# Attention scores: the keys' low-part product on all 128 rows, against tiles whose other half is zeros

## The chip, the cores and the metric

The kernel runs on one core of one Trainium2 chip. The core has a matrix engine (TensorE, PE in the profile, its weight loads listed as PEld), a vector engine (VectorE, DVE), a scalar engine (ScalarE, ACT), GpSimd (POOL) and a queue that issues transfers (SyncE, SP). The metric is the device time of one launch in microseconds (us), less is better. Before the change it is 1499.1 us, the median of three runs (1493.78 to 1500.56).

## The reference

A two-layer decoder trunk for 512 tokens of width 1024 with 16 learned meta tokens in front, so 528 positions. Layer 0 mixes an mLSTM head group and an RG-LRU branch; layer 1 is differential attention with 8 heads; a squared-ReLU MLP follows each layer. The change lies in the scores of layer 1:

```python
C_HEADS = D_MODEL // 128           # 8
C_QK_DIM = D_MODEL // (2 * C_HEADS)  # 64
Q_BLOCK = 128

def _diff_attend(qb, q_pos, kh, vh, k_pos, lam):
    """qb: (B,H,2,Lq,d), kh: (B,H,2,Lk,d), vh: (B,H,Lk,dv)."""
    s = jnp.einsum('bhcqd,bhckd->bhcqk', qb, kh)
    mask = k_pos[None, :] <= q_pos[:, None]
    p = jax.nn.softmax(jnp.where(mask, s, -jnp.inf), axis=-1)
    pd = p[:, :, 0] - lam * p[:, :, 1]
    return jnp.einsum('bhqk,bhkv->bhqv', pd, vh)
```

Every head has two components `c`, each with its own 64 query and key features, and the score is the plain dot product over these 64 features.

## The kernel before

All products are done on values split in two: a high part that TensorE's fast float format holds exactly, and the low part that is left. A product of two float32 values is then the sum of high x high, low x high and high x low. Weights come in 225 units of 128 x 1024 (`get_w`): a transfer, a cast to the high part on ScalarE (L157) and a subtraction for the low part on VectorE or, for a few units, GpSimd (L113). `unit_mm` (L188) multiplies a unit by the activations, three products for each of 8 blocks of rows.

Layer 1 goes head by head. `attend(hd)` runs three units for each head: queries, keys, values. Queries and keys get the rotary step (`raw`, `sh`, L740 to L743) and are split into `rh` and `rl` by `split` (L116 for the cast, and the subtraction by the helper at L113). Both components of a head lie on the 128 partitions, 64 each. Transfers then build for each component `c` a tile `st2[c]` of 128 rows: for queries the high part in the component's own half and the low part in the other half; for keys the high part in both halves. So one 128-row product of `qS[c]` and `kS[c]` (L792) gives high x high plus low x high. What is missing is the query's high part times the key's low part: a second product of 64 rows (L793), of the 64 rows of `qS[c]` that hold the query's high part and the 64 rows of `rl` of the keys that hold the component's low part. On the diagonal block a third product adds the causal mask (L796, `idr` times `mkr`, 128 columns). All three add up in one PSUM tile `psc`. VectorE takes the row maximum from it (`mx`, L798), turns it into the bias `nb` (L803), and ScalarE makes the exponentials (`e`, L806) which ends the use of `psc`.

A query block `I` of 128 queries sees 16 + 128 (I + 1) keys, so the score products have 144, 272, 400 or, in two parts, 2 x 264 columns. With two components that is 10 groups of products in each head, 2 of 144, 2 of 272, 2 of 400 and 4 of 264 columns, and 8 of them have the mask product.

The steps of a head (`s0` to `s3` scores, `t0` to `t3` transposes of the probabilities, `v` transposes of the values, `o` output, `f` its norm) are put between the units of the next two heads (`SLOTS`); the order within an engine is set by a scheduler that takes steps by priority groups. PSUM tiles of these steps come from a pool of four (`axp`); scratch rows come from a pool of 31 (`sc`).

Of the kernel before, what the change touches and what calls it, by code (L numbers as in the profile page):

```python
# [10 lines left out]
F32 = mybir.dt.float32  # L11
F32R = mybir.dt.float32r
# [4 lines left out]
P = 128  # L17
T = 528
# [24 lines left out]
# layer 0 before its output projection, in order: units of head h (q<h><i>: query, key and value blocks), the gate  # L43
# unit e, output-gate units o<c>, RG-LRU input and gate units c<b> and g<b>; steps without a unit: squares S and
# statistics N of the norm, gate rows A B C, RG-LRU gates G<b> and recurrences R<pair>; p<n>: n steps of the heads
# [7 lines left out]
# elementwise steps that GpSimd takes instead of VectorE  # L53
POOL_OPS = "Mm"
# weight units, by place in the order, whose low parts GpSimd computes
POOL_L = {5, 33, 43, 44, 52, 126, 140, 143, 149, 151, 155, 159, 161, 164}
N_S = 31
LOAD1 = 9
BOOST = 568
# groups of steps that come before what was emitted a little earlier  # L60
# [18 lines left out]
def trunk(tc, hT, wu, wri, pk, lv, rope, gf, out, probe=None):  # L79
    nc = tc.nc  # L80
# [6 lines left out]
    with ctx:  # L87
# [14 lines left out]
        def sc(name, dt=F32, w=T):  # L102
            """scratch row block"""
            return big.tile([P, T], dt, tag="s", name=name, bufs=N_S)

        def xt(name):
            """a pair of float32r tiles for an exact split"""
            hi = big.tile([P, T], F32R, tag="x", name=name + "h", bufs=32)
            lo = big.tile([P, T], F32R, tag="x", name=name + "l", bufs=32)
            return hi, lo  # L110
# [35 lines left out]
        def emit_load():  # L146
# [9 lines left out]
            with soon():  # L156
                nc.scalar.copy(wh, raw)  # L157
                eng = nc.gpsimd if i in POOL_L else nc.vector
                if u == U_GATE:
                    # few columns: their low parts lie beside them  # L160
                    hi, r = (a.rearrange("p (k c) -> p k c", k=KB) for a in (wh, raw))
                    sub(eng, hi[:, :, 64:100], r[:, :, 0:36], hi[:, :, 0:36].bitcast(F32))
                else:
                    sub(eng, wl, raw, wh.bitcast(F32))
# [10 lines left out]
        def unit_mm(u, x, lo=0, n=T, mid=None):  # L175
            """128 output features x n tokens, K = 1024."""
# [15 lines left out]
        # steps that follow a unit's own evacuation, emitted between later units  # L192
# [9 lines left out]
        def rsq_of(dst, v, fn, le=False, after=None, src=None):  # L202
            """dst = 1/sqrt(v): a table's value and one Newton step. src: where v comes from, as (sum, scale)."""
# [20 lines left out]
        def norm_x(h, gc, lo, tag, late=False):  # L224
            """x = h*g split exactly, and the squares of h summed over feature blocks."""
# [19 lines left out]
        def norm_r(terms, lo, tag, le=False):  # L245
            """rstd = 1/sqrt(mean(h^2)+eps) on all partitions."""
# [12 lines left out]
        # half of log1p(y) for y in [0, 1], as atanh(y/(2+y))  # L259
# [14 lines left out]
        # =================== layer 0: mLSTM heads ===================  # L274
# [16 lines left out]
        # rows on their way to another layout  # L291
# [6 lines left out]
        # column spans of the five decay blocks, packed in three rows  # L298
# [23 lines left out]
        def head_steps(hd, qk, vr):  # L322
            """the head's quadratic form, in steps"""
# [59 lines left out]
            # numerator and denominator; tokens in two spans  # L383
# [55 lines left out]
        def gate_rows():  # L439
            # gate pre-activations  # L440
# [10 lines left out]
            # columns of rstd by token block  # L451
# [11 lines left out]
        def gate_a():  # L463
            """log sigmoid of the forget gates, spread over the partitions"""
# [11 lines left out]
        def gate_b():  # L476
            """rows of the decay exponents"""
# [36 lines left out]
        # =================== layer 0: RG-LRU and output projection ===================  # L514
        # -8*softplus(-lambda) and its negative
# [106 lines left out]
        # output projection: the RG-LRU half while the last head finishes, then the mLSTM half  # L622
# [25 lines left out]
        # =================== squared-ReLU MLP ===================  # L648
# [27 lines left out]
        # =================== layer 1: differential attention ===================  # L676
# [4 lines left out]
        # lambda  # L681
# [15 lines left out]
        # causal mask of a diagonal block (query partition, key free)  # L697
# [15 lines left out]

        steps = []

        def slot(hd, i):
            """the steps that follow the unit: of head hd - 1 and, primed, of head hd - 2"""
# [5 lines left out]
        def attend(hd):  # L723
# [3 lines left out]
            for w in range(2):  # L727
# [16 lines left out]
                hl_ = (sc("rh", F32R), sc("rl", F32R))  # L744
                with pri("S"):
                    split(hl_, raw[:, lo:], slice(lo, T))
                # by component: the high part in its own half; the query's low part, or the key's high part again,
                # in the other half
# [5 lines left out]
                rot.append((st2, hl_[1]))  # L754
# [9 lines left out]
        def attn_steps(hd, rot, vr):  # L764
            (qS, _), (kS, kL) = rot
# [13 lines left out]
            def sstep(I):  # L779
# [4 lines left out]
                for c in range(2):  # L784
                    pr = slice(64 * c, 64 * c + 64)
# [5 lines left out]
                    for r, (d, s0, m) in enumerate(spans):  # L791
                        nc.tensor.matmul(d[:, :m], qS[c][:, qs], kS[c][:, s0:s0 + m], start=True, stop=False)  # L792
                        nc.tensor.matmul(d[:, :m], qS[c][pr, qs], kL[pr, s0:s0 + m], start=False,  # L793
# [83 lines left out]
        # output projection: heads 0-5 while the last heads finish, then heads 6-7  # L877
# [19 lines left out]
        # =================== last MLP and the final norm, tokens on partitions at the end ===================  # L897
# [4 lines left out]
        def turn_h(t):  # L902
            """the residual of 128 tokens, transposed"""
# [8 lines left out]
        def final_quarter(a):  # L912
            w = [get_w(N_UNIT - 8 + k) for k in range(KB)]
            for t in range(4):
                tk = slice(NM + t * P, NM + (t + 1) * P)
                turn_h(t)
                # spans of features; the first tokens go through the weights as they come
# [37 lines left out]
def lay_out(x, meta_tokens, norm_mix, norm_mlp, norm_final, ab_w_in, ab_if_bias, mlstm_norm, lru_conv_w, lru_conv_b,  # L955
# [63 lines left out]
    # rotary tables, from the shapes alone  # L1019
# [28 lines left out]
```

## Time and profile before

The profiled execution has a span of 1495.0 us from its first to its last instruction, 4.1 us under the median of the three runs.

| what | value |
|---|---|
| median of the runs | 1499.1 us |
| span of the profiled execution | 1495.0 us |
| TensorE busy | 1470.7 us, 98% |
| VectorE busy | 832.2 us, 56% |
| ScalarE busy | 634.8 us, 42% |
| GpSimd busy | 125.2 us, 8% |
| TensorE's mean granted clock | 0.993 |
| first and last score product (L792) | 856.6 us and 1083.9 us |

Shares over the whole span mix stages: VectorE, at 56% on average, is busy for eight tenths or more of most slices of the attention heads. In a timeline each row is an instruction or a run of equal ones, with its start and how long it is recorded; since matmuls overlap, what one costs is read from the start of one row to the start of the next.

### The profile page before, as it was taken

How to read it: one execution, taken by the hardware profiler on the slowest of the kernel's cores; microseconds unless marked ns; L12 is line 12 of the kernel's file. 1: busy time of each engine (PE TensorE's matmuls, PEld its weight loads, DVE VectorE, ACT ScalarE, POOL GpSimd, SP SyncE). 2: the span in 40 equal slices, each digit the busy share in tenths (PEclk: the TensorE clock that was granted, in tenths of full speed). 3: DMA queues.
4: the chain of work that ended last, by engine and by line, in shares of the span. 5: the costliest groups of instructions: out<-in, count | busy, mean ns of one | idle time of the engine just before them, and what ended most of it. 6: DMA issues, size and time to landing. Idle time of an engine off the chain costs nothing.

```text
span 1495.0 us, 24176 instructions
## 1 busy us (share of the span) xinstructions
PE 1470.7 (98%) x9970; PEld 1351.7 (90%) x9970; DVE 832.2 (56%) x1481; ACT 634.8 (42%) x1090; POOL 125.2 (8%) x94
## 2 busy tenths in 40 slices
PE   8999999999999999999999999999999999999998
PEld 8999999999999999999999888888777888888887
DVE  5867745667444434344344578888865434343452
ACT  6465734656334224132233445655645223132342
POOL 3000000100020000000003111111123000000001
PEclk9999999999999999999999989999999999999999
DMA  7332223232232232323223433222222323332331
GB/s 252 95 113 80 97 72 119 73 97 71 71 98 87 86 98 86 98 86 90 95 86 99 128 85 92 80 86 78 79 71 85 98 87 97 99 97 88 98 116 54
DMA packets 48794, 140.79 MB, mean 94 GB/s; under 512 B 9226, under 2 KB 10775, under 8 KB 48684
## 3 DMA queue, kind: packets, MB, share of 16 engines
q1 hardware_dynamic: 48108, 138.21, 30.3%
q8 instruction: 78, 1.28, 0.4%
q10 hardware_dynamic: 576, 1.05, 0.2%
q14 instruction: 32, 0.26, 0.1%
HBM read 128.55 MB, written 2.16 MB: 87 GB/s over the span
## 4 chain that ended last, share of the span: by engine, by line
PE 92%; DVE 3%; ACT 2%; issue 1%; DMA 1%; POOL 0%; SPq 0%; ACTq 0%; DVEq 0%; POOLq 0%
PE mm L188 76%; PE mf L927 3%; PE mo L890 3%; PE psc L793 2%; PE po L852 1%; PE pnum L391 1%; PE psc L796 1%; PE psc L792 1%; PE pg L584 1%; PE pss L373 1%; PE pt L828 1%; PE poq L862 0%; DVE wl L113 0%; PE pden L391 0%; ACT wh L157 0%
## 5 line engine op out<-in xcount | busy, mean ns | idle before, releaser
L157 ACT CAST wh<-raw 128x1024 fp32r<-128x1024 f32 x225 | 236.3, 1051 | 624.6 <-PE mm L188 516.0
L113 DVE TENSOR_TENSOR wl<-raw,wh 128x1024 fp32r<-128x1024 f32 x210 | 267.8, 1276 | 76.8 <-ACT wh L157 75.8
L671 DVE TENSOR_TENSOR h<-mm,h 128x264 f32<-128x264 f32 (+1 forms) x88 | 41.3, 499 | 188.3 <-PE mm L188 188.3
L241 POOL TENSOR_TENSOR nsq<-nsq 128x528 f32<-128x528 f32 (+1 forms) x28 | 48.5, 1731 | 451.0 <-DVE wl L113 336.3
L660 DVE SCALAR_TENSOR_TENSOR rt<-mm,mrstd 128x264 f32<-128x264 f32 x64 | 24.7, 427 | 88.8 <-PE mm L188 88.8
L660 DVE SCALAR_TENSOR_TENSOR rt<-mm,nrstd 128x512 f32<-128x512 f32 x32 | 22.1, 692 | 79.9 <-PE mm L188 79.8
L113 POOL TENSOR_TENSOR wl<-raw,wh 128x1024 fp32r<-128x1024 f32 x14 | 33.9, 2421 | 232.0 <-ACT wh L157 190.0
L798 DVE TENSOR_REDUCE mx<-psc 128x1 f32<-128x264 f32 (+3 forms) x80 | 34.4, 434 | 23.7 <-PE psc L796 18.1
L806 ACT ACTIVATE e<-psc,nb 128x264 f32<-128x264 f32 (+3 forms) x80 | 38.2, 482 | 18.8 <-DVE nb L803 17.7
L662 ACT ACTIVATE rt<-rt 128x528 f32<-128x528 f32 (+1 forms) x64 | 40.5, 635 | 3.1 <-DVE rt L660 2.8
L741 POOL TENSOR_TENSOR qr<-qr,tb 128x512 f32<-128x512 f32 (+1 forms) x16 | 26.4, 1648 | 156.5 <-DVE nb L803 90.7
L936 POOL TENSOR_TENSOR zg<-z,gfr 128x512 f32<-128x512 f32 x4 | 5.2, 1294 | 343.2 <-DVE z L934 332.5
L631 DVE TENSOR_TENSOR h<-mm,h 128x264 f32<-128x264 f32 x32 | 12.3, 427 | 38.5 <-PE mm L188 38.5
L840 ACT CAST pp<-pt 128x128 fp32r<-128x128 f32 (+2 forms) x64 | 21.0, 343 | 28.8 <-PE pt L828 16.7
L793 PE MATMUL psc<-rl,st 64*128 64x264 f32 (+3 forms) x80 | 31.7, 397 | 0.0
L116 ACT CAST rh<-qr 128x512 fp32r<-128x512 f32 (+1 forms) x16 | 10.0, 627 | 45.3 <-DVE qr L743 42.7
L793 PEld LDWEIGHTS psc<-rl,st 64*128 64x128 f32 x80 | 14.9, 187 | 15.0 <-issue 9.7
L188 PE MATMUL mm<-ax0h,wh 128*128 128x264 f32 x98 | 22.0, 297 | 6.1 <-ACT ax0h L230 6.1
L792 PE MATMUL psc<-st,st 128*128 128x264 f32 (+3 forms) x80 | 25.3, 317 | 2.6 <-DMA st<-rh 1.5
L113 DVE TENSOR_TENSOR pp<-pt,pp 128x256 fp32r<-128x256 f32 (+2 forms) x64 | 23.6, 378 | 1.4 <-ACT pp L840 1.3
L188 PE MATMUL mm<-a6h,wh 128*128 128x264 f32 (+1 forms) x88 | 22.6, 316 | 0.0
L188 PE MATMUL mm<-a4h,wl 128*128 128x264 f32 (+1 forms) x88 | 22.6, 316 | 0.0
(799 smaller groups left out, 4781.2 us busy)
## 6 DMA issues: line engine op xcount, KB each, us to landing
raw<-wu SPq DMA_DIRECT2D x225, 512.0 KB
h<-hT SPq DMA_DIRECT2D x16, 264.0 KB
st<-rh SPq DMA_DIRECT2D x32, 132.0 KB
st<-rh SPq DMA_DIRECT2D x16, 128.0 KB
st<-rl SPq DMA_DIRECT2D x16, 128.0 KB
cb<-crow SPq DMA_DIRECT2D x4, 264.0 KB
erb<-crow SPq DMA_DIRECT2D x4, 264.0 KB
rawg<-wri SPq DMA_DIRECT2D x4, 256.0 KB
```

The costliest lines, as they stand in the source:

```text
L113: eng.tensor_tensor(out=o, in0=a, in1=b, op=ALU.subtract)
L157: nc.scalar.copy(wh, raw)
L188: nc.tensor.matmul(p[:, :m], w[:, c], xx[:, s:s + m], start=(k == 0 and j == 0), stop=(k == KB - 1 and j == len(terms) - 1))
L241: nc.gpsimd.tensor_tensor(out=fin[0][:, lo:], in0=fin[0][:, lo:], in1=sq[:, lo:], op=ALU.add)
L660: nc.vector.scalar_tensor_tensor(out=t[:, tk], in0=p, scalar=0.0, in1=rs[:, tk], op0=ALU.max, op1=ALU.mult)
L662: nc.scalar.activation(out=t[:, lo:], in_=t[:, lo:], func=AF.Square)
L671: nc.vector.tensor_tensor(out=h[:, c, tk], in0=p, in1=h[:, c, tk], op=ALU.add)
L792: nc.tensor.matmul(d[:, :m], qS[c][:, qs], kS[c][:, s0:s0 + m], start=True, stop=False)
L793: nc.tensor.matmul(d[:, :m], qS[c][pr, qs], kL[pr, s0:s0 + m], start=False, stop=s0 + m != nk)
L806: nc.scalar.activation(out=e[:, s0:s0 + m], in_=d[:, :m], func=AF.Exp, bias=nb, scale=0.125, accum_out=ss[:, c + 2 * r:c + 2 * r + 1])
L890: nc.tensor.matmul(ps, w[ww][:, b], co[k][xx][:, NM:], start=(k == ks[0] and j == 0), stop=(k == ks[-1] and j == 2))
L927: nc.tensor.matmul(pss[n][:, :m], a[k][aa][:, tk], w[k][ww][:, f0:f0 + m], start=(k == 0 and i == 0), stop=(k == KB - 1 and i == 2))
```

## The change

The 64-row product becomes a 128-row one. Six tiles `kz` (three pairs, one of each pair for each component) are set up once; the half of a tile that belongs to the other component is filled with zeros by GpSimd. For the keys the subtraction that made the 128-row `rl` is replaced by two subtractions of 64 rows, each into the component's half of its `kz` tile; the pair is `hd % 3`. The second product then takes all 128 rows of `qS[c]` and of `kz[c]`: rows of the query's low part meet zeros. Nothing else of the computation changes; the keys no longer take an `rl` tile from the scratch pool. The rest of the diff removes comments.

```diff
+N_KZ = 3
...
+        kz = [[cp.tile([P, T], F32R, name=f"kz{i}{c}") for c in range(2)] for i in range(N_KZ)]
+        for pair in kz:
+            for c in range(2):
+                nc.gpsimd.memset(pair[c][64 - 64 * c:128 - 64 * c, :].bitcast(F32), 0.0)
...
-                hl_ = (sc("rh", F32R), sc("rl", F32R))
+                hl_ = (sc("rh", F32R), None if w else sc("rl", F32R))
                 with pri("S"):
-                    split(hl_, raw[:, lo:], slice(lo, T))
+                    if w:
+                        nc.scalar.copy(hl_[0], raw)
+                        for c in range(2):
+                            own = slice(64 * c, 64 * c + 64)
+                            sub(nc.vector, kz[hd % N_KZ][c][own, :], raw[own, :], hl_[0][own, :].bitcast(F32))
+                    else:
+                        split(hl_, raw[:, lo:], slice(lo, T))
...
-                rot.append((st2, hl_[1]))
+                rot.append(st2)
...
-            (qS, _), (kS, kL) = rot
+            qS, kS = rot
+            kL = kz[hd % N_KZ]
...
-                    pr = slice(64 * c, 64 * c + 64)
...
                         nc.tensor.matmul(d[:, :m], qS[c][:, qs], kS[c][:, s0:s0 + m], start=True, stop=False)
-                        nc.tensor.matmul(d[:, :m], qS[c][pr, qs], kL[pr, s0:s0 + m], start=False,
+                        nc.tensor.matmul(d[:, :m], qS[c][:, qs], kL[c][:, s0:s0 + m], start=False,
                                          stop=s0 + m != nk)
```

TensorE, the scores of one query block in a middle head (400 columns, both components); `mm` are a unit's products, `pt` the transposes behind. Before:

```order
L188 MATMUL mm_11290<-dx7h,wl_10995 128x512
L792 MATMUL psc<-st_11085,st_10948 128x400
L793 MATMUL psc<-rl,st_10948 128x400
L796 MATMUL psc<-mkr,idr 128x128
L792 MATMUL psc<-st_11086,st_10949 128x400
L793 MATMUL psc<-rl,st_10949 128x400
L796 MATMUL psc<-mkr,idr 128x128
L828 MATMUL pt<-ident,e_11183 72x128 x2
```

and now (the lines are 13 further down, or 2 for `unit_mm`):

```order
L190 MATMUL mm_11302<-dx7h,wl_11007 128x512
L805 MATMUL psc<-st_11097,st_10960 128x400
L806 MATMUL psc<-kz_9594,st_10960 128x400
L809 MATMUL psc<-mkr,idr 128x128
L805 MATMUL psc<-st_11098,st_10961 128x400
L806 MATMUL psc<-kz_9595,st_10961 128x400
L809 MATMUL psc<-mkr,idr 128x128
L841 MATMUL pt<-ident,e_11195 72x128 x2
```

The number and the order of TensorE's instructions stay; only the moving operand of the second product is another tile. (In the first three heads some groups of score products stand a few unit products earlier or later than before.)

VectorE in the same head, from the end of the keys' rotary step (`qr`) to the split of the values (`v1l`). Before:

```order
L743 TENSOR_TENSOR qr<-qr,qs 128x528
L815 TENSOR_SCALAR e_11037<-e_11037,rs_11044 128x272
L113 TENSOR_TENSOR pp<-pt,pp 72x2x128
L817 SCALAR_TENSOR_TENSOR e_11028<-e_11028,rs_11044,e_11037 128x272
L113 TENSOR_TENSOR rl<-qr,rh 128x528
L113 TENSOR_TENSOR v1l_11117<-pv_11119,v1h_11115 72x256
```

and now:

```order
L750 TENSOR_TENSOR qr<-qr,qs 128x528
L828 TENSOR_SCALAR e_11049<-e_11049,rs_11056 128x272
L115 TENSOR_TENSOR pp<-pt,pp 72x2x128
L830 SCALAR_TENSOR_TENSOR e_11040<-e_11040,rs_11056,e_11049 128x272
L115 TENSOR_TENSOR kz_9594<-qr,rh 64x528
L115 TENSOR_TENSOR kz_9595<-qr,rh 64x528
L115 TENSOR_TENSOR v1l_11129<-pv_11131,v1h_11127 72x256
```

One subtraction of 128 rows has become two of 64, and the split of the values stands one place later.

GpSimd at the start of the program (`nsq` are sums of squares for the first norm). Before:

```order
masks.py:197 MEMSET ident 128x128
masks.py:199 ISA
masks.py:199 AFFINE_SELECT ident<-ident 128x128
L241 TENSOR_TENSOR nsq<-nsq 128x528 x7
```

and now:

```order
masks.py:197 MEMSET ident 128x128
L719 MEMSET kz_9592 64x528
masks.py:199 ISA
masks.py:199 AFFINE_SELECT ident<-ident 128x128
L719 MEMSET kz_9593 64x528
L719 MEMSET kz_9594 64x528
L719 MEMSET kz_9595 64x528
L719 MEMSET kz_9596 64x528
L719 MEMSET kz_9597 64x528
L243 TENSOR_TENSOR nsq<-nsq 128x528 x7
```

The six fills stand ahead of the first sum of squares, one of them ahead of the last step of the identity matrix.

## Rows read from the trace of the kernel before

**Rows 1.** The page's chain that ended last: shares of the span by engine.

```profile
PE 92%; DVE 3%; ACT 2%; issue 1%; DMA 1%; POOL 0%; SPq 0%; ACTq 0%; DVEq 0%; POOLq 0%
```

**Rows 2.** Busy time by stretch: stretch, its length, then each engine's busy us, TensorE's clock.

```profile
856.60:882.70 26.10, 26.08 (x135) 21.78 (x135) 17.35 (x47) 9.41 (x28) 3.10 (x2) 0.80 0.35 97
882.70:1062.70 180.00, 178.16 (x1098) 149.14 (x1097) 156.53 (x397) 103.76 (x271) 30.44 (x17) 1.00 0.31 87
1062.70:1086.00 23.30, 22.20 (x106) 16.15 (x105) 19.62 (x59) 13.10 (x39) 1.32 (x1) 1.00 0.15 46
```

**Rows 3.** The page's groups: the 64-row product (busy us, mean ns, idle before).

```profile
L793 PE MATMUL psc<-rl,st 64*128 64x264 f32 (+3 forms) x80 | 31.7, 397 | 0.0
```

**Rows 4.** Timeline of TensorE, one head: start us, length us, line, output<-inputs, shapes.

```profile
971.22 0.39 PE L188 MATMUL mm<-dx2l,wh 128*128 128x512 f32 x1
971.45 0.23 PE L792 MATMUL psc<-st,st 128*128 128x144 f32 x1
971.61 0.33 PE L793 MATMUL psc<-rl,st 64*128 64x144 f32 x1
971.87 0.33 PE L796 MATMUL psc<-mkr,idr 128*128 128x128 f32 x1
972.03 0.45 PE L188 MATMUL mm<-dx2h,wl 128*128 128x512 f32 x1
...
996.01 0.28 PE L792 MATMUL psc<-st,st 128*128 128x264 f32 x1
996.23 0.39 PE L793 MATMUL psc<-rl,st 64*128 64x264 f32 x1
996.54 0.33 PE L796 MATMUL psc<-mkr,idr 128*128 128x128 f32 x1
996.70 0.34 PE L792 MATMUL psc<-st,st 128*128 128x264 f32 x1
996.97 0.38 PE L793 MATMUL psc<-rl,st 64*128 64x264 f32 x1
997.28 0.51 PE L188 MATMUL mm<-dx6h,wl 128*128 128x264 f32 x2
```

**Rows 5.** Timeline of TensorE: 128-row products of 256 and 128 columns.

```profile
988.49 0.28 PE L852 MATMUL po<-pp,v1l 128*128 128x256 f32 x1
988.61 0.33 PE L852 MATMUL po<-pp,v1h 128*128 128x128 f32 x2
988.78 0.28 PE L852 MATMUL po<-pp,v1l 128*128 128x128 f32 x1
988.89 0.39 PE L828 MATMUL pt<-ident,e 128*72 128x128 f32 x2
```

**Rows 6.** Timeline of TensorE: a product of 72 rows, 512 columns.

```profile
986.79 0.39 PE L852 MATMUL po<-pp,v1l 72*128 72x512 f32 x1
```

**Rows 7.** What VectorE waited for, 882.7 to 1062.7: us in total, times, longest.

```profile
DVE mx L798 <- PE psc L796: 11.3, 21, 0.8
DVE mx L798 <- PE psc L793: 3.8, 6, 1.2
```

**Rows 8.** VectorE's groups, 882.7 to 1062.7: the keys' subtraction (busy us, mean ns).

```profile
L113 DVE TENSOR_TENSOR rl<-qr,rh 128x528 fp32r<-128x528 f32 x6 | 4.2, 699 | 0.3 <-ACT rh L116 0.3
```

**Rows 9.** What TensorE's weight loads waited for, 840 to 1090: total us, times, longest.

```profile
PEld psc L792 <- DVE v1l L113: 0.5, 2, 0.2
```

**Rows 10.** Timeline of GpSimd at the start; idle time before and its releaser in brackets.

```profile
0.71 0.20 POOL masks.py:197 MEMSET ident<- 128x128 f32 x1 [0.29 <-POOLq L1039]
...
14.27 1.34 POOL L241 TENSOR_TENSOR nsq<-nsq 128x528 f32<-128x528 f32 x1 [12.98 <-ACT nsq L239]
```

**Rows 11.** Timeline of TensorE in the first head's scores.

```profile
856.62 0.30 PE L792 MATMUL psc<-st,st 128*128 128x144 f32 x1 [1.48 <-DMA st<-rh]
...
864.65 0.64 PE L188 MATMUL mm<-dx4l,wh 128*128 128x264 f32 x2
865.09 0.64 PE L188 MATMUL mm<-dx4h,wl 128*128 128x264 f32 x2
```

## The prediction, made before the change was run

> **What bounds the kernel now.** I read the chain that ended last first: TensorE carries 92% of it [rows 1]. So the question is what TensorE does in the stage of the change, and whether anything else is close behind. The busy times by stretch answer the second part [rows 2]. The stage runs from the first score product at 856.6 us to about 1086 us. In its middle, 180.0 us with the scores of six heads, TensorE is busy for 178.2 us, and VectorE for 156.5 us, 87%. In the first stretch (26.1 us) VectorE has 17.4 us of work, in the last (23.3 us) 19.6 us. TensorE is the bound, but VectorE has little room in the middle.
>
> For the first part the page's groups name the product that is replaced: 80 of them, 397 ns each as recorded [rows 3]. A recorded length holds time in which the neighbours run as well, so I take distances from start to start [rows 4]. A group with 144 columns starts at 971.45; its second product comes 0.16 us later, the mask product 0.26 after that, and the next unit product 0.16 after that: 0.58 us in all. A group with 264 columns and mask goes 0.22, 0.31 and 0.16: 0.69. One with 264 columns without a mask goes 0.27 and 0.31: 0.58.
>
> What would products of 128 rows need? A 256-column product of 128 rows is followed by the next after 0.12 us (988.49 to 988.61), and products of 128 columns follow each other after 0.085 to 0.11 us, although each of them has a weight load of its own [rows 5]. So the 64-row product costs about 0.31 us where a 128-row one of its width costs 0.12, and its neighbour in front pays too. Fewer rows alone don't do it: a 72-row product of 512 columns is recorded with the same 0.39 us [rows 6] as a 128-row one, the first row of the timeline [rows 4]. Something happens on the way from 128 to 64 rows and back, about 0.1 us on the way in and 0.2 us on the way out.
>
> The Trainium skill has a rule for this: TensorEngine Tiling (Array Packing), section Key Properties, says that a change of tiling mode drains the engine, and its list of modes has one of 64 rows and none of 72. The rows agree: 64 rows pay, 72 don't.
>
> **The change, part by part.**
>
> *TensorE.* With 128 rows all along I take 0.12 us for a product of 264 or 272 columns and 0.11 us for one of 128 or 144 columns, the upper end of [rows 5]. A 144-column group then takes 3 x 0.11 = 0.33 and saves 0.25 us. A masked group of 264 columns takes 0.12 + 0.12 + 0.11 = 0.35 and saves 0.34; without a mask 0.24, and saves 0.34. Groups of 272 and 400 columns have the same steps with a longer stream on either side, so I give them 0.34 as well. A head has ten groups, two of 144 columns: 2 x 0.25 + 8 x 0.34 = 3.2 us, 25.8 us over eight heads. The zeros cost nothing by themselves, since the number of columns stays. The weight load of the second product takes 128 rows instead of 64; [rows 5] has such loads in its distances.
>
> *VectorE.* One subtraction of 0.70 us for the keys [rows 8] becomes two. No row has it on 64 partitions; the bounds are 0.35 us each, so nothing added, and 0.70 us each. A subtraction goes along the 528 columns whatever the partitions are, so I take the second: 0.7 us more for each head. Queued behind it is the split of the values (`v1l`), which gives back PSUM tiles that the last score step takes; TensorE's weight loads already waited for it, 0.5 us in two places [rows 9]. So 0 to 0.7 us for each head can come back as a wait of TensorE.
>
> *Who is late next.* In the middle stretch TensorE would need 180.0 - 6 x 3.2 = 160.8 us. VectorE would have 156.5 + 6 x 0.7 = 160.7 us of work, and can't be busy without a gap. Of its 23.5 us of idle time 11.3 + 3.8 = 15.1 us ended with score products [rows 7]; those waits shrink as TensorE gets faster. The other 8.4 us are waits for other engines and small gaps. If all of them stay, the stretch ends at 180.0 - 15.1 + 4.2 = 169.1 us, a gain of 10.9. If they close as well it is TensorE's 160.8, a gain of 19.2. I take the middle, 15.0 us, since both lie as near: neither the waits for scores will vanish nor will the other gaps all stay.
>
> *The first and the last stretch.* In the first VectorE has 8.7 us to spare, so TensorE's 3.2 us come through. Its clock is at 0.80 of full speed there on average, which means that some 40% of the stretch runs at 1.2 instead of 2.4 GHz [rows 2], and a pair of 264-column products takes 0.44 us (864.65 to 865.09) [rows 11] against 2 x 0.12. Four groups at that clock would save up to 1.8 times as much, 1.1 us more. I take 3.8 (3.2 to 4.3). In the last stretch no key is split, VectorE has 3.7 us to spare; I take 2.6 (2.1 to 3.2).
>
> *GpSimd and the rest.* A fill of 128 columns takes 0.20 us, so one of 528 at most 0.83 us, and six 5.0 us. They run while GpSimd sits idle for 13 us before its first sum of squares at 14.27 us [rows 10]: nothing. Without that cover it would be up to 5.0 us. VectorE and GpSimd may get into each other's way in these first microseconds, when the first low parts are made; no row shows that for fills, I bound it by 0 and 0.7 us (one subtraction [rows 8]) and take 0.4. ScalarE's cast and all transfers stay as they are: the keys' tiles `st` are built from the high part alone, and don't wait for the new subtractions. A `kz` pair is written again three heads later, when its products are long done, so this wait costs nothing.
>
> *The sum.* 3.8 + 15.0 + 2.6 - 0.4 = 21.0 us, from 16.2 - 0.7 = 15.5 up to 26.7. The profiled execution's span of 1495.0 us would become 1474. The median of the three runs lies 4.1 us above that span, and I take the gain off the median: 1499.1 - 21.0 = 1478.
>
> **The rivals.**
>
> *TensorE alone sets the time*, and VectorE closes its gaps. All of 26.7 us come through: 1472. For it speaks that nearly two thirds of VectorE's idle time are waits for scores [rows 7], and that VectorE's lag is taken up by tiles in stock. Against it: it would need VectorE at 100% for 160 us.
>
> *VectorE sets the pace and hands its lag on.* The gaps stay (10.9 us in the middle) and each of six heads pays the 0.7 us behind the added subtraction: 10.9 - 4.2 + 3.2 + 2.1 = 12.0, so 1487. For it: `v1l` is already waited for [rows 9] and now stands one place later. Against: these waits are short and rare so far.
>
> *The product costs what it did*, and the change doesn't do what it says: the time goes with columns, not with rows, and the distances of [rows 4] come from something else at this place. Then 1499, between 1495 and 1504 with the 0.7 x 6 us of VectorE. Against it: [rows 5] has no such distances between products of 128 rows with changing weights. A rule of the Trainium skill speaks for it: TensorE: Matmul & The Clock Gate, section Why this matters for your kernels, says of a single product with fewer rows (32) that it takes the time of a full one, by which the swap would gain nothing. The rows agree for 72 rows and disagree for 64.
>
> *Slower: the clock falls in every head.* Ahead of the first score product TensorE waited 1.48 us for a transfer [rows 11], and in that stretch 10.4 us ran at 1.2 GHz, where a pair takes 0.44 us instead of 0.24, so 0.45 us are lost for each. If a late VectorE makes TensorE wait like that in each head, the clock may fall each time. To end 7.5 us above today, 21 + 7.5 = 28.5 us must be lost, 63 us at the low clock or six such stretches; then 1507. Against it: in the 180 us of the middle TensorE already waited 1.8 us in all, and the clock stayed at 1.00 [rows 2].
>
> **How the numbers follow.** About 0.5%, 7.5 us, is what a measurement of this kernel can tell from no change. The forecast, 1478 with 1474 to 1484 as its own range, has 0.52; TensorE alone (1472) 0.20; VectorE handing on its lag (1487) 0.15; no effect (1499) 0.08; slower (1507) 0.05. The likeliest case gives 1478. For 8 in 10 the range takes in the forecast, the lagging VectorE with 3 us of scatter, and most of the case of TensorE alone: 1470 to 1490. The first three cases end under 1491.6, so faster has 0.87, the same 0.08, slower 0.05.
>
> **What would show it right or wrong.** Right: the second product of the scores has 128 rows, its mean falls from 397 ns to that of the first, and a masked 264-column group takes 0.35 us from start to start. The middle stretch, from the second head's first score product to the eighth's, shrinks from 180 to about 165 us; VectorE is busy for 95% or more of it and waits for scores for under 6 us. TensorE shows new waits for VectorE or for the exponentials behind it, some microseconds in sum. The stages ahead of 856 us keep their length. Wrong: distances between score products as before (no effect); a stretch of 161 us with no waits of TensorE (TensorE alone); a granted clock under 0.9 in the middle stretch (slower); or a start of the program that is over 1 us later.

## The result, and the profile after

The changed kernel takes 1484.4 us (median of 5 runs, 1484.0 to 1485.1) against 1497.5 us (median of 5 runs of the kernel before, 1491.7 to 1500.6; the 1499.1 us from which the forecast started are the median of the first three of them). The ratio is 0.991, with a 95% interval of 0.989 to 0.993. The span of the profiled execution falls from 1495.0 to 1481.9 us, by 13.1. Faster by 0.9%, inside the range, but with 13.1 us where 21.0 were forecast.

The group of the second product first. The columns are busy us, mean ns of one, and idle time of the engine before them with its releaser.

```profile
L805 PE MATMUL psc<-st,st 128*128 128x264 f32 (+3 forms) x80 | 26.6, 333 | 7.2 <-DVE v1l L115 3.6
L806 PE MATMUL psc<-kz,st 128*128 128x264 f32 (+3 forms) x80 | 24.0, 300 | 0.0
```

The second product has 128 rows, and its mean falls from 397 ns [rows 3] to 300. On the right of the first row stands what is new: 7.2 us in which TensorE sat idle before a first product, half of it for `v1l`.

Now the stages of [rows 2] in the changed kernel (stretch, length, busy us of TensorE, its weight loads, VectorE, ScalarE, GpSimd, then TensorE's clock):

```profile
856.60:877.10 20.50, 19.38 (x136) 17.97 (x137) 17.45 (x47) 9.20 (x27) 3.13 (x2) 1.00 0.43 109
877.10:1050.40 173.30, 161.07 (x1097) 144.71 (x1096) 162.24 (x405) 101.20 (x271) 30.07 (x17) 1.00 0.32 92
1050.40:1073.00 22.60, 20.73 (x110) 17.51 (x110) 19.71 (x60) 13.53 (x39) 1.73 (x1) 0.92 0.15 47
```

The cuts are the same as before: the first score product of the first, the second and the eighth head. The first head's starts at 856.6 us in both kernels, so nothing was lost or won ahead of it. The first stretch went from 26.1 to 20.5 us (5.6 less), the middle from 180.0 to 173.3 (6.7 less). From the eighth head's first score product to the start of the last one of all, 21.2 us became 20.3 (0.9 less), and behind that 411 us follow in both. The sum is 13.2, the 13.1 of the span up to rounding.

In the middle TensorE's busy time is 161.1 us, as the costing said it would be, 160.8. But the stretch lasts 173.3 us. Here is what TensorE waited for in those 173 us (total us, times, longest):

```profile
PE pt L841 <- ACT e L819: 3.9, 3, 1.8
PE psc L805 <- DVE v1l L115: 3.6, 6, 0.7
PE poq L875 <- ACT osq L870: 2.3, 3, 1.8
PE pt L841 <- DVE vr L774: 1.5, 1, 1.5
PE po L865 <- ACT e L819: 0.6, 2, 0.3
PE psc L805 <- DVE pp L115: 0.4, 1, 0.4
```

These are 12.3 us; before, its busy time left 1.8 us of the middle [rows 2]. VectorE's waits turned round at the same time:

```profile
DVE mx L811 <- PE psc L809: 2.6, 7, 0.4
DVE rqa L221 <- ACT rqa L220: 2.4, 6, 0.4
DVE v1l L115 <- ACT v1h L790: 1.9, 7, 0.5
```

Its waits for scores were 15.1 us [rows 7] and are 2.6.

The timeline of one head shows the products and such a wait (start us, length us, line, output<-inputs, shapes, idle time before and its releaser):

```profile
984.57 0.28 PE L805 MATMUL psc<-st,st 128*128 128x264 f32 x1
984.69 0.28 PE L806 MATMUL psc<-kz,st 128*128 128x264 f32 x1
984.81 0.28 PE L190 MATMUL mm<-dx6h,wh 128*128 128x264 f32 x1
...
986.02 0.36 PE L805 MATMUL psc<-st,st 128*128 128x264 f32 x1 [0.69 <-DVE v1l L115]
986.22 0.28 PE L806 MATMUL psc<-kz,st 128*128 128x264 f32 x1
986.34 0.22 PE L809 MATMUL psc<-mkr,idr 128*128 128x128 f32 x1
986.40 0.34 PE L805 MATMUL psc<-st,st 128*128 128x264 f32 x1
```

And VectorE in the same microseconds:

```profile
983.15 1.41 DVE L115 TENSOR_TENSOR kz<-qr,rh 64x528 fp32r<-64x528 f32 x2
984.59 0.62 DVE L115 TENSOR_TENSOR v1l<-pv,v1h 72x256 fp32r<-72x256 f32 x2
985.45 0.42 DVE L115 TENSOR_TENSOR v1l<-pv,v1h 128x256 fp32r<-128x256 f32 x1 [0.24 <-ACT v1h L790]
```

Without a mask the group takes 984.57 to 984.81, 0.24 us where it took 0.58 [rows 4]. The next group of scores in order has to wait 0.69 us: the two subtractions for `kz` run 0.70 us each, and behind them in VectorE's queue stands the split of the values, the reader that gives back the PSUM tiles of `pv`. The score product at 986.02 needs one of those.

### The profile page after: what moved, and what is told of

It is laid out like the page before. It is cut to its first block, busy times and chain, and to the rows that moved or that the text cites. A ratio compares the mean times of both kernels' runs of the same rounds, so it can differ in the third digit from the quotient of the medians.

```text
span 1481.9 us, 24188 instructions
## 1 busy us (share of the span) xinstructions
PE 1445.6 (98%) x9970; PEld 1344.5 (91%) x9970; DVE 837.7 (57%) x1489; ACT 631.9 (43%) x1090; POOL 126.7 (9%) x100
## 4 chain that ended last, share of the span: by engine, by line
PE 85%; DVE 8%; ACT 3%; issue 2%; DMA 1%; POOL 0%; SPq 0%; DVEq 0%; ACTq 0%
PE mm L190 73%; PE mf L940 3%; PE mo L903 3%; PE pnum L393 1%; PE pss L375 1%; PE pg L586 1%; DVE wl L115 1%; DVE qr L750 1%; DMA st<-rh 1%; DVE kz L115 1%; PE pt L841 1%; DVE mx L814 1%; PE po L865 1%; PE psc L805 1%; DVE qs L747 1%
## 5 line engine op out<-in xcount | busy, mean ns | idle before, releaser
L805 PEld LDWEIGHTS psc<-st,st 128*128 128x128 f32 x80 | 15.3, 192 | 14.9 <-ACT e L819 5.3
L806 PE MATMUL psc<-kz,st 128*128 128x264 f32 (+3 forms) x80 | 24.0, 300 | 0.0
L841 PE MATMUL pt<-ident,e 128*72 128x128 f32 (+1 forms) x112 | 18.3, 278 | 5.7 <-ACT e L819 4.2
L190 PE MATMUL mm<-a1h,wh 128*128 128x264 f32 (+1 forms) x88 | 22.5, 316 | 0.0
```

Source lines behind the costliest of these rows:

```text
L190: nc.tensor.matmul(p[:, :m], w[:, c], xx[:, s:s + m], start=(k == 0 and j == 0), stop=(k == KB - 1 and j == len(terms) - 1))
```

## The experiments

The question was where the rest of the saving went. One theory, V in what follows, is that VectorE is the limit: it has more work (162.2 us in a stretch of 173.3) and the 0.7 us more in each head cost the difference. The other is that the limit is an order: scores, transposes, values and the output share four PSUM tiles (`axp`), TensorE takes its products in a fixed order, and waits where the reader of one tile is late, whoever it is (theory T, and P for the tiles, in what was expected). "Middle" is always from the first score product of the second head to that of the eighth; its start and end are each kernel's own. Diffs are against the changed kernel, where nothing else is said.

**64 rows, with all else of the change kept.**

```diff
-nc.tensor.matmul(d[:, :m], qS[c][:, qs], kL[c][:, s0:s0 + m], start=False,
+nc.tensor.matmul(d[:, :m], qS[c][64*c:64*c+64, qs], kL[c][64*c:64*c+64, s0:s0 + m], start=False,
```

> All of the change stays (zero tiles, two subtractions, fills) but the second score product takes 64 rows again, of the same tiles. If the gain comes from the 128 rows alone, the masked 264-column group goes back from 0.30 to 0.69 us, TensorE's 28 us of the products come back and VectorE's 0.7 us for each head no longer matter: 1497 to 1501 us. If the gain came from elsewhere (the keys' tiles, the pools, the order), it stays near 1484.

1496.2 us (10 runs), against 1497.5 of the kernel before on the same chip; ratio 1.000, 0.998 to 1.002. The second product's group, and the middle:

```profile
L806 PE MATMUL psc<-kz,st 64*128 64x264 f32 (+3 forms) x80 | 31.0, 387 | 0.0
```

```profile
879.00:1060.70 181.70, 179.19 (x1097) 149.12 (x1095) 162.40 (x403) 103.30 (x271) 30.58 (x17) 1.00 0.30 86
```

With the same zeros, tiles and subtractions, 64 rows give the whole gain back. So the number of rows is what gains. With TensorE as slow as it was, the middle is 1.7 us longer than before (181.7 against 180.0), with 5.9 us more of VectorE's busy time in it.

**72 rows for one of the two components.** Rows 0 to 72 hold the component's 64 rows and 8 of the zeros.

```diff
+rows = slice(0, 72) if c == 0 else slice(0, P)
-nc.tensor.matmul(d[:, :m], qS[c][:, qs], kL[c][:, s0:s0 + m], start=False,
+nc.tensor.matmul(d[:, :m], qS[c][rows, qs], kL[c][rows, s0:s0 + m], start=False,
```

> The changed kernel with component 0's second product on 72 rows (64 and 8 of zeros) and component 1's on 128. If a 64-row shape is special and not the number of rows as such, the 72-row products cost what the 128-row ones cost: 0.12 us for 264 columns from start to start, 1484. If fewer rows cost in general: half of the lost time back, about 1490.

1483.9 us (one run), a middle of 174.4 us, and among the second products, with the shapes kept apart, these of 264 columns:

```profile
L807 PE MATMUL psc<-kz,st 72*128 72x264 f32 x16 | 4.6, 286 | 0.0
L807 PE MATMUL psc<-kz,st 128*128 128x264 f32 x16 | 4.5, 283 | 0.0
```

286 ns with 72 rows and 283 with 128, in one trace; the same width took 384 ns with 64 rows in the kernel before. Forty products with 72 rows cost what 128 cost; it is the step to 64 that costs. The rule on changes of tiling mode that the prediction took from the Trainium skill (TensorEngine Tiling (Array Packing), Key Properties) has these two runs with it. The other one (TensorE: Matmul & The Clock Gate, Why this matters for your kernels) speaks of a single product, which no run here measures; among products of 128 rows, 72 rows took the same time here and 64 did not.

**Less work for VectorE: the scaling of `e` by ScalarE.** 24 operations of some 0.4 us leave VectorE in the middle.

```diff
-pool_or_dve("0123"[I]).tensor_scalar(out=es[1][:, :nk], in0=es[1][:, :nk], scalar1=rs2[:, 1:2], ...)
+nc.scalar.activation(out=es[1][:, :nk], in_=es[1][:, :nk], func=AF.Copy, scale=rs2[:, 1:2])
```

> The changed kernel, with the scaling of the second component's probabilities (L828, four for each head, 1.6 us together) on ScalarE instead of VectorE. Theory V, VectorE sets the pace of the middle heads: the middle stretch shrinks from 173 to 162 to 166 us, total 1474 to 1478. Theory T, TensorE's new waits are the latency of the score chain through ScalarE and the four PSUM tiles, whatever VectorE's load: no gain or slower, 1484 to 1489, since ScalarE gets 2 us more for each head.

1483.3 us (4 runs), ratio to before 0.990, 0.986 to 0.994. The middle:

```profile
878.20:1051.60 173.40, 162.10 (x1099) 144.72 (x1097) 153.07 (x380) 111.93 (x295) 29.14 (x17) 1.00 0.32 91
```

VectorE is busy for 153.1 us, 9.2 less, and the stretch has 173.4 us, as in the changed kernel. VectorE's gaps grew by as much: it now waits 5.3 us for the exponentials before `rs`. This speaks against theory V in its simple form, VectorE's load as a sum, but the run doesn't take load away alone: ScalarE, which makes the exponentials, got 10.7 us more (111.9 against 101.2).

**The same load in another place: each subtraction for `kz` issued twice.**

```diff
 sub(nc.vector, kz[hd % N_KZ][c][own, :], raw[own, :], hl_[0][own, :].bitcast(F32))
+sub(nc.vector, kz[hd % N_KZ][c][own, :], raw[own, :], hl_[0][own, :].bitcast(F32))
```

> The changed kernel with each of the keys' two subtractions issued twice: 1.4 us more of VectorE in each head, nothing else. Theory V: 8 to 10 us more, 1492 to 1494. Theory T: under 2 us more, 1484 to 1486.

1493.9 us (10 runs), 9.5 us more than the changed kernel; middle 182.7 us, 9.4 more, with 169.3 us of VectorE in it and a granted clock of 0.98. What TensorE waited for there, the first two rows:

```profile
PE psc L806 <- DVE v1l L115: 12.2, 6, 2.2
PE poq L876 <- ACT osq L871: 2.3, 3, 1.6
```

The wait for `v1l` grew from 3.6 to 12.2 us, by 1.4 us in each of six heads, which is what was added. So 9 us moved from VectorE to ScalarE at another place gained nothing in the middle, and 1.4 us a head put in front of `v1l` cost 1.4 us a head. The place matters.

**The change's split by transfer.** The keys are split as before, in one subtraction on 128 partitions, and two transfers bring the halves of `rl` to `kz`.

```diff
-if w: ...  (cast, two subtractions to kz)
+split(hl_, raw[:, lo:], slice(lo, T))
 ...
+nc.sync.dma_start(out=kz[hd % N_KZ][c][own, :].bitcast(F32), in_=hl_[1][own, :].bitcast(F32))
```

> The changed kernel with one 128-row subtraction for the keys as before the change, and two transfers for each head that bring its halves into the zero-padded tiles. VectorE has 0.7 us less in each head. Theory V: 4 to 5 us less than 1484.4, so 1479.5 to 1480.5, and the waits of the score products for the values' split shrink. Theory T: 1484 as before.

1481.1 us (1479.4 to 1483.4, 4 runs), ratio 0.989, 0.986 to 0.992: the lowest time of all, though its interval overlaps that of the changed kernel. VectorE is busy for 153.6 us in the middle, 8.6 less, and the wait for `v1l` is gone from TensorE's waits there:

```profile
PE pt L839 <- ACT e L817: 2.0, 2, 1.8
PE poq L873 <- ACT osq L868: 1.8, 1, 1.8
PE pt L839 <- DVE e L828: 1.8, 2, 0.9
PE mm L190 <- DVE pp L115: 1.4, 1, 1.4
```

The middle is 169.6 us, 3.7 less than in the changed kernel, but it isn't the same work: the second head's scores begin later among the unit products, so that 1067 products fall into the middle instead of 1097 and 167 instead of 136 into the first stretch, which is 3.1 us longer. From the first score product to the last it takes 213.5 us, against 214.1. So with the wait for `v1l` and 8.6 us of VectorE's work gone, the stage of the scores gains 0.6 us as traced. Its middle ran at a granted clock of 0.99, that of the changed kernel at 1.00; even if this cost the full 1.7 us, not all of the 3.6 us came back. Most of the 2.4 us by which the span is shorter lies ahead of the scores, whose first product comes at 854.9 us instead of 856.6, where TensorE does the same work in both. Theory V had 4 to 5 us; the medians differ by 3.3, and no more than 0.6 of that shows in the stage of the scores.

**The same subtractions behind the values' split.** An order between instructions, no wait, puts the two subtractions of a head behind the three of `v1l`; the load stays.

```diff
+k = sub(nc.vector, kz[hd % N_KZ][c][own, :], raw[own, :], hl_[0][own, :].bitcast(F32))
+for v in last_v[-3:]:
+    tc.add_manual_dep(k.ins, v.ins.name, ... "order")
```

> The changed kernel with the keys' two subtractions moved behind the split of the values on VectorE (v1l), in every head; load and counts unchanged. If the place is what costs (the PSUM tiles of the values come free later, and the last score step of a head waits for them, 3.6 us in all in the changed kernel's trace): those waits go to zero and the time falls by 3 to 6 us to 1479 to 1481. If VectorE's load alone sets the pace: no change, 1484 to 1485.

1482.6 us (4 runs); ratio 0.990, 0.988 to 0.991; 1479 to 1481 were expected. The middle is longer, 176.9 us, with a granted clock of 0.98 in it. From the first score product to the last product of the output projection, between which both kernels do the same work, it takes 253.4 us as in the changed kernel: nothing is gained in the stage as traced, and the span's 1.1 us less lie ahead of the scores. TensorE's waits from 840 to 1090 us:

```profile
PE psc L810 <- DVE rqy L885: 6.4, 4, 2.0
PE poq L880 <- ACT osq L875: 2.6, 2, 2.4
...
PE psc L810 <- DVE v1l L115: 0.3, 1, 0.3
```

`v1l` falls to 0.3 us, but the next product of scores now waits 6.4 us for `rqy`. That operation is the last of the output's norm, and it reads the output tile `po`, another of the four PSUM tiles. The wait moved from one holder of a tile to the next; what made `rqy` late stands at the end of this section.

**A fifth tile.** Five tiles for the attention and three for the units, in place of four and four.

```diff
-mmp = ... bufs=4
-axp = ... bufs=4
+mmp = ... bufs=3
+axp = ... bufs=5
```

> The changed kernel with five PSUM tiles for the attention steps instead of four, and three instead of four for the unit products. If TensorE's new waits are for these tiles (score and transpose steps that wait for exponentials and for the values' split), most of their 8 us go and the time falls to 1476 to 1480. If VectorE's load sets the pace: 1483 to 1485. If three tiles are too few for the units: slower, over 1490.

1494.2 us (10 runs). With three tiles for the units 15.6 us are lost ahead of the scores, whose first product comes at 872.2 us; the middle itself is 167.9 us, 5.4 shorter, with VectorE at 160.5 us:

```profile
897.50:1065.40 167.90, 162.19 (x1094) 146.24 (x1092) 160.53 (x404) 98.99 (x269) 28.92 (x16) 0.99 0.33 95
```

Not all of the 5.4 us are the tile's. In the changed kernel the first eight products of the output projection (`mo`, 0.23 us each from start to start) stand in the last 3 us of the middle; here seven of them come behind it, 1.6 us. Some 3.8 us are left for the fifth tile.

**The output tile from the units' pool.** `po` leaves the four, which frees one at times, and takes one of the units' four.

```diff
-po = st["po"] = axt("po")
+po = st["po"] = mmt("po")
```

> The changed kernel with the output tile (po, held from step o to step f) in the pool of the unit products, so that scores, transposes and values have the four PSUM tiles to themselves. Theory P, the four tiles hand VectorE's and ScalarE's lag on to TensorE: the middle stretch falls from 173 to 167 to 169 us, the total to 1478 to 1480. Theory V, VectorE's load alone: 1484.

1484.2 us (5 runs). The middle is 168.5 us, 4.8 less, and the total doesn't move. All eight `mo` products, 1.8 us, come behind this middle, so that 3.0 us of the 4.8 can be the tile's. The middle is the one that theory P named, the total the one of theory V. In the last heads, 1045 to 1075 us, TensorE waits:

```profile
PE pt L841 <- DVE e L830: 5.5, 1, 5.5
PE psc L805 <- DVE nb L816: 0.7, 1, 0.7
```

In the changed kernel the `mo` products start at 1047.4 us, among the steps of the last head. Here they need a tile of the pool in which `po` sits, start at 1058.4, and leave a hole of 5.5 us.

The same edit was made to the kernel before, and together with two of the variants above:

> The kernel before with the same move of the output tile and the 64-row product as it was. By theory P the tiles bind only once TensorE is fast: TensorE waited 1.8 us in the middle stretch, so at most 2 us of gain, 1490 to 1498 as the kernel before. If more tiles help as such: 5 us or more below the kernel before of the same chip.

> Both moves: the keys' subtractions behind the values' split, and the output tile in the other pool. The wait for the output tile's release (6.4 us in the run with the first move alone) goes by theory P: 1475 to 1478. By theory V 1482 as with the first move alone.

> The low part by transfer (0.7 us less of VectorE in each head, 1481.1 alone) and the output tile in the other pool. By theory P the two add up, 1474 to 1477; TensorE's own need of the middle stretch, some 150 to 161 us, is not reached, since VectorE has about 157 us of work there. If the tiles don't matter: 1481.

| kernel, each with `po` in the units' pool | us, median | middle, us | VectorE in it | the hole in the last head, us |
|---|---|---|---|---|
| changed kernel | 1484.2 | 168.5 | 160.8 | 5.5 |
| kernel before | 1502.2 | 177.0 | 156.4 | 4.7 |
| subtractions behind the values | 1485.2 | 168.1 | 157.7 | 4.5 |
| split by transfer | 1488.1 | 168.3 | 153.8 | 5.5 |

The middle of the kernel before shrinks by 3.0 us and that of the changed one by 4.8; without the eight `mo` products, which stand in both middles and come later in all four rows, it is 1.2 and 3.0. The middle of the last row can't be set beside the others, since it has 1058 products to their 1089 and 1090. The lower three rows are slower than the same kernels without the move, by 5.7, 2.6 and 7.0 us, and the first is level; 1502 us for the kernel before, and 1485 and 1488 for the combinations, lie outside what was expected. Around the hole TensorE's granted clock fell: between the first and the last score product of the last head it was 0.81, 0.76, 0.73 and 0.67 in the four rows, and 0.92, 1.00, 1.00 and 0.92 in the same kernels without the move.

**The kernel before, once more.**

> The kernel before, unchanged, for its clock run by run: 1490 to 1501 us with a mean clock of 0.990 to 0.996. If the scatter of its runs (11 us) is the clock, the slow runs have the lower mean clock, about 0.001 for each 1.5 us, and the trace of a run near 1491 has no stretch of 10 us at 1.2 GHz at the first head's scores.

1493.9 us (1490.9 to 1501.5, 10 runs) beside 1497.0 (1489.7 to 1500.8, 19 runs) of the same program. Its times spread over 11 us, those of the changed kernel over 1.2. The spread goes with TensorE's mean granted clock in the run, by 1.1 us for each 0.001 where 1.5 were expected (mean us, runs; levels 0.991, 0.993, 0.997 and 0.999 are left out; the second and third columns rest on one or two runs each):

| mean clock of the run | kernel before | changed kernel | 64 rows on `kz` |
|---|---|---|---|
| 0.990 | 1500.9 (6) | | |
| 0.992 | 1498.7 (16) | | |
| 0.994 | 1496.1 (15) | 1485.0 (2) | 1498.4 (2) |
| 0.995 | | 1484.3 (2) | 1496.5 (2) |
| 0.996 | 1492.8 (9) | 1484.0 (1) | 1496.0 (1) |
| 0.998 | 1491.4 (5) | | 1493.5 (2) |
| 1.000 | 1490.1 (5) | | |

At the same mean clock the change gains 8.8 us (0.996) to 11.1 us (0.994), and the 128 rows by themselves, changed kernel against the 64 rows, 12.0 to 13.4. The last part of what was expected was not tested, since the traced execution is one of 1498.6 us and not one near 1491. In the profiled executions one long stretch at the low level stands out, in the first head of the kernel before (first row) and its repetition (second row), and not in the changed one (third) or that with 64 rows on `kz` (fourth):

```profile
859.00:869.20 10.20, 10.20 (x36) 8.13 (x36) 5.75 (x19) 1.56 (x4) 1.77 (x1) 0.51 0.18 43
```

```profile
859.00:869.20 10.20, 10.20 (x39) 7.74 (x40) 5.78 (x19) 1.57 (x4) 1.78 (x1) 0.57 0.09 21
```

```profile
859.00:869.20 10.20, 9.88 (x80) 9.51 (x79) 9.21 (x27) 5.39 (x16) 2.46 (x2) 1.00 0.34 87
```

```profile
859.00:869.20 10.20, 10.20 (x70) 8.75 (x70) 8.46 (x27) 5.38 (x16) 1.79 (x1) 1.00 0.27 57
```

The fourth has the old product and no dip, and its first stretch, 22.2 us to the second head, is 1.7 us longer than that of the changed kernel. So of the 5.6 us of the first stretch about 1.7 belong to the products and about 4 to the clock. TensorE's busy time in it is 2.8 us less with 128 rows (19.4 against 22.2); 1.1 of them came back as waits.

The last head has the clock in it as well. From its first score product to its last one the changed kernel takes 20.3 us at 0.92 and the kernel before 21.2 at 1.00; its repetition ran there at 0.92 too:

```profile
1062.60:1085.30 22.70, 21.60 (x94) 15.60 (x94) 17.98 (x55) 12.53 (x37) 1.32 (x1) 0.92 0.15 47
```

At the same granted clock the gain there is 2.4 us and not 0.9.

**What stands ahead of the longest waits: a reading of the traces, without a run.** In the changed kernel four of TensorE's waits in the middle last 1.5 us or more, together 6.7 of its 12.3 us, and a fifth follows in the last head. Ahead of each, GpSimd subtracts for a unit's low part `wl`, and an operation of VectorE lasts until that subtraction ends, or once 0.6 us longer. One of the five:

```profile
989.99 2.38 POOL L115 TENSOR_TENSOR wl<-raw,wh 128x1024 fp32r<-128x1024 f32 x1 [9.48 <-ACT wh L159]
990.37 2.02 DVE L814 TENSOR_TENSOR mx<-mx 128x1 f32<-128x1 f32 x1
993.44 0.41 PE L841 MATMUL pt<-ident,e 128*72 128x128 f32 x2 [1.59 <-ACT e L819]
```

The median of this `mx` is 0.15 us. Two places behind it in VectorE's queue stands the bias `nb` that ScalarE needs for the exponentials `e`, and with these TensorE's wait ends.

| `wl` on GpSimd ends at | VectorE's operation | its length, us | it ends at | TensorE's wait behind it, us |
|---|---|---|---|---|
| 905.67 | `mx` | 1.98 | 905.68 | 1.51 |
| 934.58 | `mx` | 1.96 | 934.60 | 1.75 |
| 992.37 | `mx` | 2.02 | 992.38 | 1.59 |
| 1012.27 | `qr` (L750) | 2.90 | 1012.83 | 1.80 |
| 1052.13 | `mx` | 2.02 | 1052.15 | 1.87 |

The kernel before has long operations at four of these places too, 1.54 to 2.90 us, but TensorE's waits behind them are 0.5 to 1.1 us. With the subtractions behind the values, each of the four waits for `rqy` comes behind an operation of that norm (L221 or L223) that lasts 2.4 to 2.9 us beside such a `wl`, where the others of its line take 0.7. That GpSimd holds VectorE up is read from times that coincide; a run with these low parts made elsewhere would test it, and there is none.

## Why the prediction was right, and where it was not

*The price of the product* held. The group without a mask was put at 0.24 us and takes 0.24. The masked one of 264 columns was put at 0.35; the timeline above has 0.20 + 0.12 + 0.06 = 0.38 behind the wait, and one of 272 columns that didn't wait takes 0.31:

```profile
972.54 0.29 PE L805 MATMUL psc<-st,st 128*128 128x272 f32 x1
972.66 0.29 PE L806 MATMUL psc<-kz,st 128*128 128x272 f32 x1
972.79 0.22 PE L809 MATMUL psc<-mkr,idr 128*128 128x128 f32 x1
972.85 0.34 PE L190 MATMUL mm<-dx5h,wl 128*128 128x264 f32 x1
```

TensorE's need in the middle, 160.8 us, came as 161.1 busy. That the rows are the reason, and that 72 would do as well, two runs show.

*VectorE's price* held: 0.70 us for a subtraction on 64 partitions, the upper of its bounds. So did the warning on `v1l`: 3.6 us in six heads are 0.6 a head, of the 0 to 0.7 that were named.

That the time fell inside the range owes something to luck: two errors had opposite signs. The middle fell 8.3 us short, and about 4 us came from the clock of the first stretch, where the sum had 0.6. Without them the gain would have been near 10 us, which is close to the edge of the range.

*The middle was the mis-sized term*: 15.0 us forecast, 6.7 measured. I took the middle between "VectorE's other gaps stay" (10.9) and "they close" (19.2); what came lies under both, for the lower one already had its waits for scores at zero. Count it by VectorE: before, 156.5 busy, 15.1 waiting for scores and 8.4 in other gaps; after, 162.2 busy, 2.6 and 8.5. The other gaps stayed, to a tenth. The waits for scores did not go to zero, which costs 2.6, and the busy time rose by 5.7 where the subtractions account for 4.2. Two groups grew beside them: 13 operations `mx` on 128x1 went from 6.8 to 9.3 us in sum and 6 scalings of `e` with 272 columns from 3.2 to 4.2, for some of them lasted as long as a GpSimd operation beside them. 169.1 + 2.6 + 1.5 + 0.1 = 173.3. That is a count and not yet a cause. The forecast took VectorE's time as a sum of work and gaps. What it named and left out of its sum is that TensorE, in its fixed order, stops behind a late VectorE. Of the 12.3 us of waits 3.6 are for `v1l`; that this place costs is shown by the doubled subtractions. What it costs in all stays open: with this wait taken away the stage of the scores took 0.6 us less (by transfer) and the same time (by order), but the lower clock of those two middles can have cost up to 1.7 and 3.5 us, 0.01 and 0.02 of their lengths, an estimate. Another 6.7 us stand behind operations of VectorE that last as long as GpSimd's subtraction, which the forecast didn't have at all at this place; that is read from the traces and not tested.

*The rival with VectorE's lag handed on* described the middle better than the forecast: its term there, 10.9 - 4.2 = 6.7, is the number measured, and its total of 1487 is nearer than 1478. The exact match is luck, for the `v1l` waits that it put at 4.2 are 3.6 of 12.3 us. Its name is half right. The lag is handed on, in part through the order at `v1l`; that VectorE simply has too much to do is not what the runs show.

*The first stretch* gained 5.6 us, forecast 3.8. The size of its parts was wrong in both directions: the products gave about 1.7, not 3.2, and the low clock, which I took as a price on the products, went away as a whole, for about 4. *The last heads* gave 0.9, not 2.6; but at the same granted clock of 0.92, against the repetition of before, it is 2.4, within what was put down. *GpSimd's fills* cost nothing that shows, since the first score product starts at the same 856.6 us; 0.4 was put down.

Of the signs named beforehand, these came true: the product's mean (300 ns beside 333 of the first one), the groups, score waits of VectorE under 6 us (2.6), new waits of TensorE, a clock of 1.00 in the middle, unchanged stages ahead of it. Not so: 165 us for the middle, and 95% for VectorE (162.2 of 173.3, 94%).

*What stays open.* No run brought the middle near TensorE's 159 to 162 us of busy time. The held operations of VectorE are the candidate that the traces show for what is left, without a run that moves them. And whether the change is the reason for the missing low clock in the first head isn't shown. All three traces with the old order of VectorE's work have the dip (before, its repetition, and before with `po` moved), the 64-row kernel with all else changed doesn't. But the dip alone lowers the mean clock of a run to 0.997, and 13 of 70 runs of the kernel before had 0.998 or more, so it does not come in every run of that kernel.

## What to carry to other kernels

A product of 64 rows between products of 128 was dear for its neighbours here as well; if the other half can be zeros at the price of one more VectorE operation, or the rows can be 72, take that. Then ask, before counting the gain, which tiles the faster engine will ask for earlier, and what stands in the queue in front of the reader that frees them: here work added there came back in full, and work moved off VectorE elsewhere brought nothing. Taking one wait away mostly showed the next one. Compare variants over stretches that hold the same instructions and at the same granted clock: several gains here were in part instructions that had moved out of the stretch.

## What the hardware showed that was not expected

- A VectorE subtraction on 64 partitions with 528 columns takes 0.70 us, as on 128 [rows 8]: the row of the timeline above has two in 1.41 us. A split by partition halves doubles its time.
- The mask product right behind the second one is followed by the next product after 0.06 us, half of what I had taken from [rows 5], in the two masked groups shown above.
- The kernel before is 10.8 us slower at a mean granted clock of 0.990 than at 1.000. The spread of 11 us between its runs goes with TensorE's clock. At the same mean clock this change gains 8.8 to 11.1 us, where the medians say 13.1; which of the two is the change's own depends on whether it is the reason for its clock, and that is open.
- An operation of VectorE on 128x1 elements that takes 0.15 us as a rule was recorded with 1.96 to 2.02 us four times in the changed kernel, each time ending within 0.02 us of a GpSimd subtraction of 128x1024.
